# Second attention of a decoder layer: transposes of q, k and the attention weights go from TensorE to VectorE and ScalarE

## The chip, the cores and the metric

The kernel runs on one core of a Trainium2 chip. The metric is the time of one execution on the device, in microseconds. One of the executions is recorded by the hardware profiler; it gives the profile and the trace. The engines have short names: PE is TensorE's matmul, PEld its weight load, DVE is VectorE, ACT is ScalarE, POOL is GpSimd and SP issues most of the DMAs.

## The reference, cut to what matters

One hybrid decoder layer in float32, with 256 positions, a width of 2048 and 8 heads in each of two attentions. The change is in the second attention alone. Its block length equals the sequence length, so no other block is ever chosen, and what is left is causal attention with ALiBi:

```python
x = x + 0.5 * swiglu(rmsnorm(x, g_ffn1), w_ffn1_gu, w_ffn1_down)
h = rmsnorm(x, g_mix)
qa, ka, va, qb, kb, vb, gate_a, gate_b = split(h @ w_in)      # 3*1024, 3*1024, 2048, 2048 columns
o_a = diff_attention(qa, ka, va, lam, ...)                    # the first attention, 8 heads
# moba_attention, the second: per head of 128 columns, for this shape
s = q @ k.T * 128 ** -0.5                                     # 256 x 256
s = where(dist >= 0, s - slope * dist, -inf)
o_b = softmax(s) @ v
merged = sigmoid(gate_a) * (o_a @ p_a) + sigmoid(gate_b) * (o_b @ p_b)
x = x + merged @ w_o
x = x + 0.5 * swiglu(rmsnorm(x, g_ffn2), w_ffn2_gu, w_ffn2_down)
return rmsnorm(x, g_final)
```

## The kernel before, in words

The 256 positions lie in two tiles of 128 partitions. Each large product (`products`) streams its weight matrix from HBM in blocks of 512 columns. Every float32 weight tile `raw` is split into a high part `wh` (a copy by ScalarE, L103) and a low part `wl` (a difference by VectorE, L104), two row tiles of 128 at a time, and three matmuls per row tile and position tile add up in PSUM (L131 to L133). So one pair `wh`, `wl` feeds 12 matmuls. There are four `wh` buffers and three `wl` buffers, so ScalarE can run four pairs ahead of TensorE, and VectorE three. The text counts the work in these pairs.

The small work of the attentions is put between the matmuls of the large products. A queue `work` holds functions; `products` runs one of them after every fourth row tile (every two pairs), except at the start of a product. A product of 2048 rows has 8 pairs and three such steps. The framework's scheduler then orders each engine's instructions; an engine runs its list in order, and `wh` and `wl` are put forward by a priority.

In the steps around the change:
- While the q and k columns of the second attention are computed (`qkv`, four products for q and k), the eight heads of the first attention run in the steps. After each of these four products VectorE scales 512 columns into `qk`, and a piece of work is put at the head of the queue: `put_rows` transposes `qk` by eight TensorE transposes (`flipped`, L178) into PSUM tiles `tr`, and ScalarE copies them to their place (L214). The piece has 4 heads of q or k.
- Each head of the first attention (`diff_head`) takes four steps: scores and softmax; transpose of the weights `a`; the product with v, `o`, whose rows ScalarE scales to `on` (L343); and a transpose of `on`, which ScalarE and VectorE split into `oah` and `oal`. `tr` and `o` share two PSUM buffers: the transposes of `a` use the buffer that `oal` must have read.
- While the gate columns are computed, the eight heads of the second attention run (`moba_head`). In step i TensorE does the scores `sc` of head i, and two steps later the product `o` with v. In between VectorE adds ALiBi and takes the maxima (`s`, `top`, L304 to L308), ScalarE does the exponentials (L312), and VectorE takes `inv` and scales the weights to `a` (L359, L362). In the next step three TensorE transposes and one ScalarE copy (`flip_weights`, L178 and L319) make `aT`. After `o` ScalarE and VectorE split it into `obh` and `obl`. `sc` has one PSUM buffer, `aT` and `a` have two.

Elsewhere the kernel already transposes by VectorE: `turned` makes a full transpose of 128x512 from 16 transposes of 32x256, each from one group of 32 partitions to another (L193).

Of the kernel before, what the change touches and what calls it, by code (L numbers as in the profile page):

```python
# [24 lines left out]
F32 = mybir.dt.float32  # L25
F32R = mybir.dt.float32r
AF = mybir.ActivationFunctionType
# [3 lines left out]
P = 128  # L31
S = 256
T = S // P
# [4 lines left out]
Q = 32  # L38
# [9 lines left out]
def layer(ctx: ExitStack, tc: tile.TileContext, x_in, g_ffn1, w_gu1, w_down1, g_mix, w_in, lam_q1,  # L48
          lam_k1, lam_q2, lam_k2, g_subln, p_a, p_b, w_o, g_ffn2, w_gu2, w_down2, g_final, out):
    nc = tc.nc  # L50
    keep = ctx.enter_context(tc.tile_pool(name="keep", bufs=1))
    wp = ctx.enter_context(tc.tile_pool(name="wp", bufs=1))
    tp = ctx.enter_context(tc.tile_pool(name="tp", bufs=1))
# [46 lines left out]
    def split(hi, lo, src, scale=None):  # L100

        if scale is None:
            a = nc.scalar.activation(hi, src, AF.Copy)  # L103
            b = nc.vector.tensor_tensor(lo, src, hi.bitcast(F32), op=ALU.subtract)  # L104
        else:
            a = nc.scalar.activation(hi, src, AF.Copy, scale=scale)  # L106
            b = nc.vector.scalar_tensor_tensor(lo, src, scale, hi.bitcast(F32), op0=ALU.mult, op1=ALU.subtract)
        return a.ins, b.ins
# [61 lines left out]
    def product(lhs, w, n0, nk, apart=0):  # L170
        return products(lhs, w, [n0], nk, apart=apart)[0]

    def flipped(src):

        n = src.shape[-1] // P
        tr = psum.tile([P, n * P], F32, name="tr", tag="tr", bufs=2)
        for i in range(n):
            nc.tensor.transpose(tr[:, i * P:(i + 1) * P], src[:, i * P:(i + 1) * P], ident)  # L178
        return tr

    def both_tiles(name):

        return tp.tile([P, T, NB], F32, name=name, tag="h", bufs=1)
# [25 lines left out]
        i, k = divmod(k, size)  # L209
        return [part[:, k:k + n, t * P:(t + 1) * P] for part in lhs[i]]  # L210

    def put_rows(dst, both):
        for t in range(T):
            nc.scalar.activation(dst[:, :, t * P:(t + 1) * P],  # L214
                                 flipped(both[:, t]).rearrange("p (k q) -> p k q", k=4), AF.Copy)

    def put_turned_rows(dst, rows):
        for t in range(T):
# [75 lines left out]
    def weights(h, maps, qT, kT):  # L294

        n = len(maps)
        sc = psum.tile([P, n, NB], F32, name="sc", tag="sc", bufs=1)
        for m, rows in enumerate(maps):
            nc.tensor.matmul(sc[:, m, :P], qT[rows, h, :P], kT[rows, h, :P], start=True, stop=True)  # L299
        for m, rows in enumerate(maps):  # L300
            nc.tensor.matmul(sc[:, m, P:3 * P], qT[rows, h, P:], kT[rows, h, :], start=True, stop=True)  # L301
        s = tp.tile([P, n, 3 * P], F32, name="s", tag="s", bufs=2)
        slope = 2.0 ** (-8.0 * (h + 1) / HEADS)
        nc.vector.scalar_tensor_tensor(s, dist[:, None, :].to_broadcast([P, n, 3 * P]), slope, sc[:, :, :3 * P],  # L304
                                       op0=ALU.mult, op1=ALU.add)
        top = tp.tile([P, 2, n], F32, name="top", tag="top", bufs=2)
        nc.vector.tensor_reduce(top[:, 0, :], s[:, :, :P], axis=AX.X, op=ALU.max, negate=True)
        nc.vector.tensor_reduce(top[:, 1, :], s[:, :, P:], axis=AX.X, op=ALU.max, negate=True)  # L308
        total = tp.tile([P, 2, n], F32, name="total", tag="total", bufs=2)
        for m in range(n):  # L310
            for t, cols in enumerate((slice(0, P), slice(P, 3 * P))):
                nc.scalar.activation(s[:, m, cols], s[:, m, cols], AF.Exp, bias=top[:, t, m:m + 1],  # L312
                                     accum_out=total[:, t, m:m + 1])
        return s, total

    def flip_weights(a):

        aT = tp.tile([P, 3 * P], F32, name="aT", tag="aT", bufs=2)
        nc.scalar.activation(aT, flipped(a), AF.Copy)  # L319
        return aT  # L320

    def diff_head(h, qT, kT, v, lam, on, oT):
        p, total = weights(h, (slice(0, 64), slice(64, 128)), qT, kT)
        inv = tp.tile([P, T, 2], F32, name="inv", tag="inv", bufs=2)
        nc.vector.reciprocal(inv, total)

        c = tp.tile([P, T, 1], F32, name="c", tag="c", bufs=2)
        nc.vector.scalar_tensor_tensor(c, inv[:, :, 1:2], lam, total[:, :, 0:1], op0=ALU.mult, op1=ALU.mult)
        a = tp.tile([P, 3 * P], F32, name="a", tag="a", bufs=2)
        for t, cols in enumerate((slice(0, P), slice(P, 3 * P))):  # L330
            nc.vector.scalar_tensor_tensor(a[:, cols], p[:, 1, cols], c[:, t], p[:, 0, cols],
                                           op0=ALU.mult, op1=ALU.add)
        yield
        aT = flip_weights(a)
        yield
        o = psum.tile([P, T, P], F32, name="o", tag="tr", bufs=2)
        hc = slice(h * P, (h + 1) * P)
        nc.tensor.matmul(o[:, 0], aT[:, :P], v[:, 0, hc], start=True, stop=True)
        nc.tensor.matmul(o[:, 1], aT[:, P:2 * P], v[:, 0, hc], start=True, stop=False)
        nc.tensor.matmul(o[:, 1], aT[:, 2 * P:], v[:, 1, hc], start=False, stop=True)  # L340
        ss = tp.tile([P, T, 1], F32, name="oss", tag="oss", bufs=2)
        for t in range(T):
            nc.scalar.activation(on[:, t], o[:, t], AF.Copy, scale=inv[:, t, 0:1])  # L343
            sq = tp.tile([P, P], F32, name="osq", tag="osq", bufs=1)
            nc.vector.scalar_tensor_tensor(sq, on[:, t], 1.0, on[:, t], op0=ALU.mult, op1=ALU.mult,
                                           accum_out=ss[:, t])
        r = tp.tile([P, T, 1], F32, name="orms", tag="orms", bufs=2)
        nc.vector.tensor_scalar(ss, ss, 1.0 / P, EPS, op0=ALU.mult, op1=ALU.add)
        nc.gpsimd.tensor_tensor(r[:, :, 0], ss[:, :, 0], half.to_broadcast([P, T]), op=ALU.pow)
        for t in range(T):  # L350
            nc.vector.tensor_scalar(on[:, t], on[:, t], r[:, t], 1.0 - LAM_INIT, op0=ALU.mult, op1=ALU.mult)
        yield
        (hi, lo), = oT
        split(hi[:, h], lo[:, h], flipped(on.rearrange("p t d -> p (t d)")), scale=gsub)

    def moba_head(h, qT, kT, v, oT):
        p, total = weights(h, (slice(0, P),), qT, kT)
        inv = tp.tile([P, T, 1], F32, name="inv1", tag="inv", bufs=2)
        nc.vector.reciprocal(inv, total)  # L359
        a = tp.tile([P, 3 * P], F32, name="a1", tag="a", bufs=2)  # L360
        for t, cols in enumerate((slice(0, P), slice(P, 3 * P))):
            nc.vector.tensor_scalar(a[:, cols], p[:, 0, cols], inv[:, t], None, op0=ALU.mult)  # L362
        yield
        aT = flip_weights(a)
        yield
        o = psum.tile([P, S], F32, name="o1", tag="tr", bufs=2)
        hc = slice(h * P, (h + 1) * P)
        nc.tensor.matmul(o, v[:, 0, hc], aT[:, :S], start=True, stop=False)  # L368
        nc.tensor.matmul(o[:, P:], v[:, 1, hc], aT[:, S:], start=False, stop=True)  # L369
        (hi, lo), = oT  # L370
        split(hi[:, h], lo[:, h], o)

    def qkv(xT, rstd, n0, dim, tag):

        all_ = keep.tile([P, 3, HEADS * S], F32, name=f"qkv_{tag}", tag=tag)
        qT, kT = (all_[:, i].rearrange("p (h q) -> p h q", h=HEADS) for i in range(2))
        v = all_[:, 2].rearrange("p (t n) -> p t n", t=T)
        rq = []
        for t in range(T):
            rq.append(tp.tile([P, 1], F32, name="rq", tag="rq", bufs=2))  # L380
            nc.vector.tensor_scalar(rq[t], rstd[t], dim ** -0.5, None, op0=ALU.mult)
        for i, (dst, r) in enumerate(((qT, rq), (kT, rstd))):
            for b in range(W // NB):
                y = product(xT, w_in[0], n0 + i * W + b * NB, KD)
                hs = both_tiles("qk")
                for t in range(T):
                    nc.vector.tensor_scalar(hs[:, t], y[t], r[t], None, op0=ALU.mult)
                if work:
                    put_piece = partial(put_rows, dst[:, 4 * b:4 * b + 4], hs)
                else:  # L390
                    put_piece = partial(put_turned_rows, dst[:, 4 * b:4 * b + 4], turned(hs))
                work.appendleft(put_piece)
        for b in range(W // NB):
            y = product(xT, w_in[0], n0 + 2 * W + b * NB, KD)
            for t in range(T):
                nc.scalar.activation(v[:, t, b * NB:(b + 1) * NB], y[t], AF.Copy, scale=rstd[t])
        return qT, kT, v
# [155 lines left out]
```

## Time and profile before

| | us |
|---|---|
| median of three runs | 2110.7 (2110.1 to 2110.76) |
| profiled execution, its own time | 2111.54 |
| its span, first to last instruction | 2109.7 |
| PE busy in the span | 2091.8 (99%) |
| DVE busy | 1380.0 (65%) |
| ACT busy | 983.5 (47%) |

The three runs agree within 0.03%. The profiled execution is 0.84 us above the median, and its own time is 1.84 us more than its span. Matmuls are pipelined, so two that follow each other overlap in the record; the distance of their starts is what one costs the engine. Busy shares are averages over stages with different limits.

### The profile page before, as it was taken

The page shows a single profiled execution, that of the slowest core. Times are in us where ns is not written, and L with a number is a line of the kernel's source. Part 1 is how long each engine was busy: PE and PEld are TensorE (multiplying, and loading weights), DVE is VectorE, ACT ScalarE, POOL GpSimd, SP SyncE. Part 2 cuts the span into 40 slices and gives each one's busy share as a digit, 9 for nine tenths or more (in the row PEclk, how much of TensorE's full clock was granted, in tenths as well). Part 3 has the DMA queues.
Part 4 walks back from the last instruction along what each step waited for, and adds up shares of the span by engine and source line. Part 5 has one row for each costly group of instructions (what it writes and reads, how often), then busy time and mean ns, then how long its engine had stood idle before and what let it go on. Part 6 is the DMA issues. An engine that isn't in the chain of part 4 may idle for free.

```text
span 2109.7 us, 24363 instructions
## 1 busy us (share of the span) xinstructions
PE 2091.8 (99%) x9330; PEld 1729.4 (82%) x9330; DVE 1380.0 (65%) x1846; ACT 983.5 (47%) x1224; POOL 13.6 (1%) x26
## 2 busy tenths in 40 slices
PE   8999999999999999999999999999999999999998
PEld 7888888888888888778888888888888888888886
DVE  5676664466678887675554489977766644666754
ACT  6544443344445544555564534554444433444443
POOL 0000000000000000000000000000000000000000
PEclk9999999999999999999999999999999999999999
DMA  7556655565555556545545555565565556556563
GB/s 244 198 181 200 198 194 188 196 199 187 193 199 190 191 192 201 166 153 167 180 160 193 187 197 194 187 219 194 185 199 200 184 195 199 191 189 199 180 200 138
DMA packets 201799, 401.25 MB, mean 190 GB/s; under 512 B 6945, under 2 KB 6994, under 8 KB 201554
## 3 DMA queue, kind: packets, MB, share of 16 engines
q1 hardware_dynamic: 201584, 399.66, 57.3%
q8 instruction: 73, 1.20, 0.2%
q14 instruction: 44, 0.36, 0.0%
q10 hardware_dynamic: 98, 0.03, 0.0%
HBM read 397.57 MB, written 2.10 MB: 189 GB/s over the span
## 4 chain that ended last, share of the span: by engine, by line
PE 98%; ACT 1%; DVE 0%; DMA 0%; issue 0%; ACTq 0%; SPq 0%; POOLq 0%; POOL 0%; DVEq 0%
PE acc L131 32%; PE acc L133 32%; PE acc L132 32%; PE tr L178 1%; ACT wh L103 0%; DMA raw<-in_w_ffn_gu_dram 0%; PE sc L301 0%; PE o L368 0%; DVE wl L104 0%; PE sc L299 0%; ACT on L343 0%; ACT oah L106 0%; PE o L369 0%; ACT sq L243 0%; DVE rows L193 0%
## 5 line engine op out<-in xcount | busy, mean ns | idle before, releaser
L104 DVE TENSOR_TENSOR wl<-raw,wh 128x1024 fp32r<-128x1024 f32 x752 | 918.1, 1224 | 619.7 <-PE acc L132 558.2
L103 ACT ACTIVATE wh<-raw 128x1024 fp32r<-128x1024 f32 x752 | 796.6, 1060 | 914.7 <-PE acc L133 889.2
L131 PE MATMUL acc<-wh,xTh 128*128 128x512 f32 x1472 | 577.5, 393 | 2.2 <-ACT xTh L106 2.2
L133 PE MATMUL acc<-wh,xTl 128*128 128x512 f32 x1472 | 574.4, 390 | 0.2 <-DVE xTl L104 0.2
L132 PE MATMUL acc<-wl,xTh 128*128 128x512 f32 x1472 | 573.8, 390 | 0.0
L131 PEld LDWEIGHTS acc<-wh,xTh 128*128 128x128 f32 x1472 | 277.4, 188 | 60.4 <-ACT xTh L106 2.6
L133 PEld LDWEIGHTS acc<-wh,xTl 128*128 128x128 f32 x1472 | 276.9, 188 | 58.5 <-DVE xTl L104 0.6
L132 PEld LDWEIGHTS acc<-wl,xTh 128*128 128x128 f32 x1472 | 277.0, 188 | 57.0
L132 PE MATMUL acc<-wl,bigh 128*128 128x512 f32 x704 | 274.0, 389 | 0.0
L131 PE MATMUL acc<-wh,bigh 128*128 128x512 f32 x704 | 273.7, 389 | 0.0
L133 PE MATMUL acc<-wh,bigl 128*128 128x512 f32 x704 | 273.7, 389 | 0.0
L131 PE MATMUL acc<-wh,oah 128*128 128x512 f32 x416 | 161.8, 389 | 0.0
L132 PE MATMUL acc<-wl,oah 128*128 128x512 f32 x416 | 161.8, 389 | 0.0
L133 PE MATMUL acc<-wh,oal 128*128 128x512 f32 x416 | 161.8, 389 | 0.0
L131 PE MATMUL acc<-wh,obh 128*128 128x512 f32 x416 | 161.8, 389 | 0.0
L132 PE MATMUL acc<-wl,obh 128*128 128x512 f32 x416 | 161.8, 389 | 0.0
L133 PE MATMUL acc<-wh,obl 128*128 128x512 f32 x416 | 161.8, 389 | 0.0
L193 DVE STREAM_TRANSPOSE rows<-h 32x256 f32<-32x256 f32 x352 | 153.5, 436 | 6.4
L132 PEld LDWEIGHTS acc<-wl,bigh 128*128 128x128 f32 x704 | 132.2, 188 | 27.7 <-DVE wl L104 0.4
L133 PEld LDWEIGHTS acc<-wh,bigl 128*128 128x128 f32 x704 | 132.2, 188 | 27.5
L131 PEld LDWEIGHTS acc<-wh,bigh 128*128 128x128 f32 x704 | 132.2, 188 | 27.4
L133 PEld LDWEIGHTS acc<-wh,obl 128*128 128x128 f32 x416 | 78.1, 188 | 16.2
(116 smaller groups left out, 1056.5 us busy)
## 6 DMA issues: line engine op xcount, KB each, us to landing
raw<-in_w_ffn_gu_dram SPq DMA_DIRECT2D x174, 1024.0 KB, 5.1
raw<-in_w_ffn_down_dram SPq DMA_DIRECT2D x88, 1024.0 KB, 5.0
raw<-in_w_in_dram SPq DMA_DIRECT2D x80, 1024.0 KB, 5.1
raw<-in_w_o_dram SPq DMA_DIRECT2D x16, 1024.0 KB, 5.1
raw<-in_p_a_dram SPq DMA_DIRECT2D x8, 1024.0 KB, 5.2
raw<-in_p_b_dram SPq DMA_DIRECT2D x8, 1024.0 KB, 5.1
x<-in_x_dram SPq DMA_DIRECT2D x8, 256.0 KB, 5.9
raw<-in_w_ffn_gu_dram SPq DMA_DIRECT2D x4, 512.0 KB, 6.5
```

The source lines that it names most:

```text
L103: a = nc.scalar.activation(hi, src, AF.Copy)
L104: b = nc.vector.tensor_tensor(lo, src, hi.bitcast(F32), op=ALU.subtract)
L131: nc.tensor.matmul(acc[t], hi, wh, start=(k == 0), stop=False)
L132: nc.tensor.matmul(acc[t], hi, wl, start=False, stop=False)
L133: return nc.tensor.matmul(acc[t], lo, wh, start=False, stop=(k == nk - 1)).ins
L178: nc.tensor.transpose(tr[:, i * P:(i + 1) * P], src[:, i * P:(i + 1) * P], ident)
L193: nc.vector.transpose(rows[c * Q:(c + 1) * Q, a], both[a * Q:(a + 1) * Q, c])
```

## The change

For q and k of the second attention, `squares_of` replaces the eight TensorE transposes of a piece by two VectorE instructions over all 128 partitions, each of which transposes every 32x32 square in place of its group of partitions (128x512 elements, L218 after). `put_squares` then moves the squares to their partitions by 16 ScalarE copies of 32 partitions x 256 elements (L226), where there were two of 128x512 from PSUM. `squares` takes the one buffer `rows` that `turned` uses.

For the weights of the second attention, `turn_weights` makes `aT` with 16 VectorE transposes of 32 partitions x 96 elements (three squares each, L339), each from one group of partitions of `a` to another of `aT`. The three TensorE transposes and the ScalarE copy of a head are gone. The first attention keeps them.

```diff
-    def put_rows(dst, both):
-        for t in range(T):
-            nc.scalar.activation(dst[:, :, t * P:(t + 1) * P],
-                                 flipped(both[:, t]).rearrange("p (k q) -> p k q", k=4), AF.Copy)
+    def squares_of(both):
+        squares = tp.tile([P, 4, T, 4, Q], F32, name="squares", tag="rows", bufs=1)
+        for t in range(T):
+            nc.vector.transpose(squares[:, :, t], both[:, t].rearrange("p (k c j) -> p c k j", c=4, j=Q))
+        return squares
+
+    def put_squares(dst, squares):
+        for a in range(4):
+            for c in range(4):
+                part = dst[c * Q:(c + 1) * Q].rearrange("p k (t a i) -> p t k a i", t=T, i=Q)[:, :, :, a]
+                nc.scalar.activation(part, squares[a * Q:(a + 1) * Q, c], AF.Copy)
...
+    def turn_weights(a):
+        aT = tp.tile([P, 3, 4, Q], F32, name="aT", tag="aT", bufs=2)
+        a = a.rearrange("p (b c j) -> p c b j", c=4, j=Q)
+        for q in range(4):
+            for c in range(4):
+                nc.vector.transpose(aT[c * Q:(c + 1) * Q, :, q], a[q * Q:(q + 1) * Q, c])
+        return aT.rearrange("p b q i -> p (b q i)")
...
-        aT = flip_weights(a)
+        aT = turn_weights(a)
...
-                    put_piece = partial(put_rows, dst[:, 4 * b:4 * b + 4], hs)
+                    put_piece = partial(put_squares, dst[:, 4 * b:4 * b + 4], squares_of(hs))
```

Line numbers after the change are higher by 11 to 20 from `squares_of` on: L304 becomes L315, L359 becomes L379, and so on.

The first place is ScalarE at the first q piece, while heads of the first attention run. Before:

```order
L103 ACTIVATE wh<-raw 128x1024 x3
L214 ACTIVATE qkv_bigl<-tr 128x4x128 x2
L103 ACTIVATE wh<-raw 128x1024 x2
L106 ACTIVATE oah<-tr,gains 128x256
L343 ACTIVATE on<-o,inv 128x128 x2
```

Now:

```order
L103 ACTIVATE wh<-raw 128x1024 x2
L226 ACTIVATE qkv_bigl<-squares 32x2x4x32 x2
L103 ACTIVATE wh<-raw 128x1024
L226 ACTIVATE qkv_bigl<-squares 32x2x4x32 x6
L103 ACTIVATE wh<-raw 128x1024
L226 ACTIVATE qkv_bigl<-squares 32x2x4x32 x5
L103 ACTIVATE wh<-raw 128x1024
L226 ACTIVATE qkv_bigl<-squares 32x2x4x32 x3
L106 ACTIVATE oah<-tr,gains 128x256
L363 ACTIVATE on<-o,inv 128x128 x2
```

The 16 copies stand between the last `wh` before `oah`, in the second and third piece as 4, 6, 5 and 1.

The second place is VectorE at the fourth head of the second attention, from its maxima to the next head. Before:

```order
L307 TENSOR_REDUCE top<-s 128x1
L308 TENSOR_REDUCE top<-s 128x1
L104 TENSOR_TENSOR wl<-raw,wh 128x1024
L359 RECIPROCAL inv_7777<-total 128x2
L362 TENSOR_SCALAR a_7779<-s,inv_7777 128x128
L362 TENSOR_SCALAR a_7779<-s,inv_7777 128x256
L104 TENSOR_TENSOR wl<-raw,wh 128x1024
L104 TENSOR_TENSOR obl<-o_7816,obh 128x256
```

Now:

```order
L318 TENSOR_REDUCE top<-s 128x1
L319 TENSOR_REDUCE top<-s 128x1
L104 TENSOR_TENSOR wl<-raw,wh 128x1024
L379 RECIPROCAL inv_7838<-total 128x2
L382 TENSOR_SCALAR a_7840<-s,inv_7838 128x128
L382 TENSOR_SCALAR a_7840<-s,inv_7838 128x256
L104 TENSOR_TENSOR wl<-raw,wh 128x1024
L339 STREAM_TRANSPOSE aT<-a_7840 32x3x32 x3
L104 TENSOR_TENSOR obl<-o_7877,obh 128x256
L339 STREAM_TRANSPOSE aT<-a_7840 32x3x32 x13
L104 TENSOR_TENSOR wl<-raw,wh 128x1024
```

The 16 transposes stand in VectorE's list between the same `wl` as before, ahead of the next head.

The third place is TensorE at the step in which the product `o` of the third head stands. Before:

```order
L133 MATMUL acc_7720<-wh,xTl 128x512
L368 MATMUL o_7816<-aT,qkv_bigl 128x256
L369 MATMUL o_7816<-aT,qkv_bigl 128x128
L178 MATMUL tr<-ident,a_7779 128x128 x3
L299 MATMUL sc<-qkv_bigl 128x128
L301 MATMUL sc<-qkv_bigl 128x256
```

Now:

```order
L133 MATMUL acc_7770<-wh,xTl 128x512
L388 MATMUL o_7877<-aT,qkv_bigl 128x256
L389 MATMUL o_7877<-aT,qkv_bigl 128x128
L310 MATMUL sc<-qkv_bigl 128x128
L312 MATMUL sc<-qkv_bigl 128x256
```

The three transposes are gone, and each `o` stands behind as many matmuls of the large product as before.

## Rows read from the trace of the kernel before

**Rows 1.** The page, part 1: busy us, share of the span, instructions.

```profile
PE 2091.8 (99%) x9330; PEld 1729.4 (82%) x9330; DVE 1380.0 (65%) x1846; ACT 983.5 (47%) x1224; POOL 13.6 (1%) x26
```

**Rows 2.** Window: length; PE, PEld, DVE, ACT, POOL busy (instructions); clock; DMA.

```profile
900.00:920.00 20.00, 19.38 (x104) 15.64 (x103) 15.90 (x37) 12.38 (x30) 1.39 (x2) 1.00 0.39 121
```

**Rows 3.** Timeline of PE at the first q piece: start, duration.

```profile
896.39 0.40 PE L133 MATMUL acc<-wh,xTl 128*128 128x512 f32 x1
896.62 1.04 PE L178 MATMUL tr<-ident,qk 128*128 128x128 f32 x8
...
897.73 0.39 PE L132 MATMUL acc<-wl,xTh 128*128 128x512 f32 x1
```

**Rows 4.** Timeline of PE, heads of the second attention.

```profile
1025.02 0.38 PE L299 MATMUL sc<-qkv_bigl 128*128 128x128 f32 x2
...
1031.15 0.49 PE L178 MATMUL tr<-ident,a 128*128 128x128 f32 x3
...
1031.47 0.39 PE L299 MATMUL sc<-qkv_bigl 128*128 128x128 f32 x2
...
1091.22 0.59 PE L368 MATMUL o<-aT,qkv_bigl 128*128 128x256 f32 x2
...
1103.13 0.59 PE L368 MATMUL o<-aT,qkv_bigl 128*128 128x256 f32 x2
```

**Rows 5.** Groups of DVE by form: count, busy, mean ns, idle before.

```profile
L104 DVE TENSOR_TENSOR wl<-raw,wh 128x1024 fp32r<-128x1024 f32 x752 | 918.1, 1224 | 619.7 <-PE acc L132 558.2 <-issue 39.8 <-ACT wh L103 10.8
...
L104 DVE TENSOR_TENSOR bigl<-rows,bigh 128x512 fp32r<-128x512 f32 x44 | 30.2, 688 | 6.5 <-ACT bigh L103 6.5
L193 DVE STREAM_TRANSPOSE rows<-qk 32x256 f32<-32x256 f32 x64 | 27.9, 436 | 1.1
```

**Rows 6.** Timeline of DVE, at transposes and at a head's start.

```profile
454.31 2.23 DVE L193 STREAM_TRANSPOSE rows<-h 32x256 f32<-32x256 f32 x5
...
1025.05 1.23 DVE L104 TENSOR_TENSOR wl<-raw,wh 128x1024 fp32r<-128x1024 f32 x1 [1.50 <-PE acc L132]
1026.19 0.55 DVE L304 SCALAR_TENSOR_TENSOR s<-dist,sc 128x384 f32<-128x384 f32 x1
```

**Rows 7.** Window of seven heads of the second attention, columns as in rows 2.

```profile
1026.20:1086.00 59.80, 59.80 (x290) 50.39 (x289) 36.70 (x67) 40.11 (x72) 0.00 (x0) 1.00 0.51 164
```

**Rows 8.** Waits in 1020 to 1110 us: total, times, longest.

```profile
DVE inv L359 <- ACT s L312: 5.7, 8, 0.8
```

**Rows 9.** Groups of ACT by form, columns as in rows 5.

```profile
L103 ACT ACTIVATE wh<-raw 128x1024 fp32r<-128x1024 f32 x752 | 796.6, 1060 | 914.7 <-PE acc L133 889.2 <-DMA raw<-in_w_ffn_gu_dram 5.3 <-issue 5.1
...
L219 ACT ACTIVATE qkv_bigh<-rows 128x512 f32<-128x512 f32 x8 | 5.0, 625 | 14.9 <-DVE rows L193 14.9
L343 ACT ACTIVATE on<-o,inv 128x128 f32<-128x128 f32 x16 | 4.9, 361 | 0.0
```

**Rows 10.** Timeline at the step behind the first q piece.

```profile
902.97 0.38 PE L178 MATMUL tr<-ident,on 128*128 128x128 f32 x2
...
903.17 1.06 ACT L103 ACTIVATE wh<-raw 128x1024 fp32r<-128x1024 f32 x1 [1.61 <-PE acc L133]
...
904.13 0.46 ACT L106 ACTIVATE oah<-tr,gains 128x256 fp32r<-128x256 f32 x1
...
904.49 0.61 ACT L343 ACTIVATE on<-o,inv 128x128 f32<-128x128 f32 x2
904.62 0.48 DVE L107 SCALAR_TENSOR_TENSOR oal<-tr,gains,oah 128x256 fp32r<-128x256 f32 x1 [0.40 <-ACT oah L106]
...
905.15 0.55 PE L178 MATMUL tr<-ident,a 128*128 128x128 f32 x3 [0.28 <-ACT on L343]
```

**Rows 11.** Timeline of PE at the start of the kernel.

```profile
9.71 0.63 PE L133 MATMUL acc<-wh,xTl 128*128 128x512 f32 x1
10.14 0.63 PE L131 MATMUL acc<-wh,xTh 128*128 128x512 f32 x1
...
13.55 0.63 PE L133 MATMUL acc<-wh,xTl 128*128 128x512 f32 x1
```

## The prediction

> **What bounds the kernel now.** First the busy times: PE is busy for 99% of the span [rows 1], so what it no longer does is time won, and every wait put on it is time lost. Then the two stages of the change, by windows. While q and k of the second attention are computed, PE has small gaps and VectorE is the next busiest, at 15.9 of 20 us in the fullest window [rows 2]. While the heads of the second attention run, PE has no gap, and VectorE is busy for 36.7 of 59.8 us [rows 7]. Last the timelines, for what one step costs on the engine that bounds, and for how close the others are behind it.
>
> **What PE saves.** A matmul of the large products starts 0.23 us after the one before. Around the eight transposes of a piece, the step from the transposes to the second matmul behind them is 897.73 - 896.62 = 1.11 us where 0.23 would stand [rows 3]: 0.88 for eight, 3.5 us for four pieces. The three transposes of a head push the scores from 1031.15 to 1031.47 [rows 4]: 0.32, 2.6 us for eight heads. Together 6.1 us. The records show 0.33 us and more for one transpose, but they overlap, so the starts count.
>
> **The squares on VectorE.** Eight instructions of 128x512. By the rate of the rows, 1224 - 688 = 536 ns for 512 elements [rows 5], one is 436 + 256 x 1.047 = 0.70 us; two per piece, 5.6 us in all. They stand between the scaling of `qk` and the next `wl` but one, in a stage where VectorE has 4 of 20 us free [rows 2] and runs three pairs ahead. I cost them at nothing; without that cover they cost 5.6.
>
> **The copies on ScalarE.** A copy of 128x1024 takes 1060 ns and one of 128x512 625 [rows 9], so 256 columns take 0.41 us. Two `on` of 0.361 take 0.61 together [rows 10]: the second starts 0.11 before the first ends. No row has copies that change partitions; the bounds are a start every 0.30 us (they overlap like `on`) and every 0.41 (they don't). I take 0.30, for the rows of the same engine show the overlap. A piece then takes 4.8 us where about 1.06 stood. ScalarE waits 1.6 us ahead of a `wh` [rows 10], so groups of 5 and 6 copies fill these gaps, and `oah` behind them is late. Whoever waits: `oal`, then the buffer `tr`, then the transposes of `a` on PE, which already wait there from about 904.70 to 905.15 [rows 10]. By adding up ScalarE's list of the first piece from 0.65 us after the end of pair 322 (896.62), when the squares are ready (2 copies, `wh`, 6, `wh`, 5, `wh`, 3), `oah` starts at 8.4 us, `oal` ends at 9.35, and PE, which now has four matmuls ahead of the transposes, is there at 8.2. That is a wait of 1.2 where 0.45 stood. In the second and third piece one copy stands behind the last `wh`, and I get 0.1 more each; behind the fourth piece no transposes of `a` follow. Sum 1.0; since each lateness also moves `on` and the exponentials, I take 1.5. With a start every 0.41 the same addition gives 2.4 + 1.9 + 1.9 = 6.2.
>
> **The weights on VectorE: the term that decides.** 128 transposes of 32x96. A transpose of 32x256 takes 436 ns [rows 5], and five start 2.23 / 5 = 0.446 apart [rows 6]: they don't overlap, unlike the `s` that starts 0.09 before its `wl` ends [rows 6]. At the measured rate, 160 elements less are 0.168 less: 0.268, one start every 0.28 us. Bounds: proportional to the elements, 0.164 (0.174 apart), and no shorter than 32x256, 0.446 apart. I take 0.28, since `wl` and its half show a fixed part (1224 is less than twice 688). That is 4.5 us per head on an engine that has to give 1.2 us per pair besides.
>
> [...]
>
> PE needs `aT` of head 7 at its product `o`. Scores of head 1 start at 1025.02, that `o` at 1091.22 [rows 4]; without seven groups of transposes it would be due 66.2 - 2.2 = 64.0 us after them. VectorE's list up to the last transpose of head 7: `s` of head 1 starts 1.2 us in [rows 4, 6]; seven heads with 18 `wl` and six `obl` are the window's 36.7 [rows 7]; one more `wl` 1.2; 112 transposes x 0.28 = 31.4; the overlap that an instruction loses beside transposes, 0.09 at two places a head, 1.3; and waits for exponentials. Those were 5.7 over eight heads [rows 8], 5.0 for seven. Now a `wl` stands in the gap in most heads, but on ScalarE a `wh` stands between the two exponentials in several; I take half, 2.5 (bounds 0 and 5). Sum 74.3: `o` of head 7 waits until VectorE is 10.3 us behind. On the way `o` of heads 4 and 6 take part of that as waits of their own, and `sc` waits where `s` of the head before is late. Behind it PE has 11.9 - 0.3 = 11.6 us to the last `o` [rows 4] and VectorE one head with three `wl`, 2.2 + 4.5 + 3.7 + 0.5 = 10.9: no more is added.
>
> **Sum.** -6.1 + 1.5 + 10.3 = +5.7 us. The profiled execution is 2111.54 by its own time on a span of 2109.7, so its like would be 2117.2 on 2115.4. The median of the runs is 0.84 lower: 2110.7 + 5.7 = 2116.4.
>
> **Rivals.**
> - **The transposes are short and VectorE keeps up.** Nothing is late where a start comes every 0.19 us (0.28 - 10.3 / 112). At the lower bound the sum is -6.1 + 1.5 = -4.6: 2106.1. For it: nothing here is as short. Against it: the fixed part. [...]
> - **The copies don't overlap on ScalarE.** Instead of 1.5 the pieces cost 6.2: 2121.1. For it: transposes between groups of partitions don't overlap on VectorE [rows 6]. Against it: that is another engine.
> - **The transposes are long.** At 0.446 apart, 112 x 0.166 = 18.6 more: 2135.0; at 0.31, 3.4 more: 2119.8. Against it: the measured rate.
> [...]
>
> **How the numbers follow.** Chances: forecast 0.60, its own range 2113 to 2120 (waits for exponentials 0 to 5 us, transposes 15 ns either way); short transposes 0.12; copies without overlap 0.14; long transposes 0.07; the clock 0.05; 0.02 for less than I see. I count 0.2%, 4.2 us, as the least that a measurement of this kernel can tell from no change: 2106.5 to 2114.9. About a quarter of the forecast (0.16), half of the short transposes (0.06) and 0.03 of the rest fall within; 0.07 fall below it; 0.68 above. The range 2108 to 2123 leaves out 0.08 below and some 0.10 above.
>
> **What the profile after would show.** PE: no L178 for `qk`, 24 fewer for `a`; about 10 us of idle time between 1040 and 1100, before `o` of heads 4, 6 and 7, put down to transposes on VectorE (L339), whose mean is 0.27. VectorE nearly full from head 1 to 8, its total 128 x 0.27 + 5.6 = 40 us higher. ScalarE: 64 copies of 0.4. The waits of `tr<-a` behind the pieces about 1 us longer. If L339 is below 0.19, or if PE does not wait at `o`, the forecast is wrong; if `tr` waits over 2 us behind each piece, the second rival holds.

## The result, and the profile after

The changed kernel takes 2129.95 us (median of 4 runs, 2128.85 to 2131.78), the kernel before 2110.62 beside it on the same chip: 1.0091 times as long, 95% interval 1.0079 to 1.0103, 19.3 us more. The predicted direction was right; the time lies 7 us above the range.

The first part of the page of after, in the columns of [rows 1], on a span of 2128.3 us:

```profile
PE 2094.9 (98%) x9274; PEld 1728.4 (81%) x9274; DVE 1417.4 (67%) x1982; ACT 1002.2 (47%) x1272; POOL 13.6 (1%) x26
```

PE has 56 instructions less and its busy time is 3.1 us longer. Its mean granted clock over the run, by the view of the cores, is 0.995, where before had 0.999:

```profile
core 0: 2128.3 us, clock 0.995
```

Where the time went is told by windows of the two stages; columns as in [rows 2]. Before:

```profile
885.00:1010.00 125.00, 123.43 (x613) 101.11 (x613) 81.17 (x152) 66.54 (x126) 5.54 (x8) 1.00 0.49 158
1010.00:1130.00 120.00, 120.00 (x559) 100.36 (x559) 65.00 (x95) 71.41 (x110) 0.00 (x0) 1.00 0.52 172
```

After:

```profile
885.00:1010.00 125.00, 115.00 (x536) 92.53 (x536) 80.13 (x154) 85.06 (x177) 5.53 (x8) 0.96 0.43 143
1010.00:1130.00 120.00, 113.12 (x498) 92.99 (x497) 94.61 (x220) 61.37 (x95) 0.00 (x0) 0.97 0.48 158
...
900.00:920.00 20.00, 16.41 (x83) 12.73 (x83) 11.34 (x30) 14.48 (x36) 1.39 (x2) 0.91 0.32 107
```

The first stretch holds q and k of the second attention beside the heads of the first, the second the heads of the second. PE is idle for 10 and for 6.9 us in them (before 1.6 and 0), and beside that the granted clock is 0.96 and 0.97. The last row is the stretch of [rows 2], where the clock was 1.00.

The waits of PE in the first stage and (below the dots) in the second, from the view of waits of after (total us, times, longest):

```profile
PE tr L178 <- ACT on L363: 9.5, 5, 3.2
PE tr L178 <- DVE on L371: 0.5, 1, 0.5
...
PE o L388 <- DVE aT L339: 5.8, 2, 2.9
PE sc L310 <- DVE s L315: 1.1, 2, 0.9
```

In before the first of these lines was

```profile
PE tr L178 <- ACT on L343: 1.5, 5, 0.3
```

(the 0.28 of [rows 10] is one of its five), and the other three had nothing. In after three of the five are long, one behind each of the first three pieces (3.25, 2.77 and 2.77 us by the timeline). The 0.5 us of the second line is a wait of the transposes of `on` behind the fourth piece. The timeline of PE at the first, after:

```profile
908.16 0.61 PE L178 MATMUL tr<-ident,a 128*128 128x128 f32 x3 [3.25 <-ACT on L363]
908.47 0.74 PE L132 MATMUL acc<-wl,xTh 128*128 128x512 f32 x1
909.00 0.63 PE L133 MATMUL acc<-wh,xTl 128*128 128x512 f32 x1
909.43 0.63 PE L131 MATMUL acc<-wh,xTh 128*128 128x512 f32 x1
...
911.56 0.57 PE L133 MATMUL acc<-wh,xTl 128*128 128x512 f32 x1
911.97 0.39 PE L131 MATMUL acc<-wh,xTh 128*128 128x512 f32 x1
912.20 0.39 PE L132 MATMUL acc<-wl,xTh 128*128 128x512 f32 x1
```

Behind the wait the matmuls start 0.43 us apart, as at the start of the kernel [rows 11], and go back to 0.23 at 911.97. The granted clock of 900 to 920 is 0.91: the wait is paid twice.

What the wait is for stands in ScalarE's timeline of after, to be read beside [rows 10]:

```profile
902.62 2.12 ACT L226 ACTIVATE qkv_bigl<-squares 32x256 f32<-32x256 f32 x5
904.76 1.06 ACT L103 ACTIVATE wh<-raw 128x1024 fp32r<-128x1024 f32 x1
905.84 1.26 ACT L226 ACTIVATE qkv_bigl<-squares 32x256 f32<-32x256 f32 x3
907.12 0.47 ACT L106 ACTIVATE oah<-tr,gains 128x256 fp32r<-128x256 f32 x1
907.49 0.62 ACT L363 ACTIVATE on<-o,inv 128x128 f32<-128x128 f32 x2
```

Five copies take 2.12 us, three 1.26: a start every 0.43, and even the `wh` starts 0.02 after the last copy has ended. `oah` starts at 907.12 and the transposes of `a` end their wait 1.04 later.

The heads of the second attention, to be read beside [rows 4], in PE's timeline of after: the scores of head 1, the `o` of head 7 and that of head 8.

```profile
1035.14 0.38 PE L310 MATMUL sc<-qkv_bigl 128*128 128x128 f32 x2
...
1108.44 0.70 PE L388 MATMUL o<-aT,qkv_bigl 128*128 128x256 f32 x2 [2.88 <-DVE aT L339]
...
1121.74 0.59 PE L388 MATMUL o<-aT,qkv_bigl 128*128 128x256 f32 x2
```

The `o` of head 7 waits for VectorE's transposes, which last as long as reckoned, by the view of L339 in after (in ns the least, the median and the most):

```profile
L339 DVE STREAM_TRANSPOSE aT<-a x128: 255/270/276, 1040.2 to 1119.4; 32x96 f32<-32x96 f32 x128
```

The scores of head 1 now start 10.1 us later; from there to the last `o` it is 86.6 us, 8.5 more. Together that is the 18.6 us by which the spans of the two profiled executions differ (2128.3 and 2109.7), so the rest of the kernel takes as long as before. Each part comes out of three numbers, to within 0.6 us. First stage: 3.5 saved, 8.5 more waiting (9.5 and 0.5, against 1.5), and 125 x 0.04 = 5.0 of clock: +10.0. Second: 2.6 saved, 6.9 waiting, 120 x 0.03 = 3.6 of clock: +7.9.

### The profile page after: what moved, and what is told of

Read it like the earlier page. It is cut to its first block, busy times and chain, and to the rows that moved or that the text cites. A ratio compares the mean times of both kernels' runs of the same rounds, so it can differ in the third digit from the quotient of the medians.

```text
span 2128.3 us, 24423 instructions
## 1 busy us (share of the span) xinstructions
PE 2094.9 (98%) x9274; PEld 1728.4 (81%) x9274; DVE 1417.4 (67%) x1982; ACT 1002.2 (47%) x1272; POOL 13.6 (1%) x26
## 4 chain that ended last, share of the span: by engine, by line
PE 94%; ACT 2%; DVE 2%; issue 0%; DMA 0%; ACTq 0%; POOL 0%; SPq 0%; POOLq 0%; DVEq 0%
PE acc L131 31%; PE acc L132 31%; PE acc L133 31%; ACT qkv_bigl L226 1%; DVE aT L339 1%; ACT wh L103 1%; DVE wl L104 1%; PE tr L178 0%; DMA raw<-in_w_ffn_gu_dram 0%; PE sc L312 0%; ACT on L363 0%; ACT oah L106 0%; PE sc L310 0%; DVE s L315 0%; PE o L388 0%
## 5 line engine op out<-in xcount | busy, mean ns | idle before, releaser
L132 PEld LDWEIGHTS acc<-wl,obh 128*128 128x128 f32 x416 | 78.1, 188 | 16.2
```

The costliest lines, as they stand in the source:

```text
L132: nc.tensor.matmul(acc[t], hi, wl, start=False, stop=False)
```

## The experiments

**The two halves.** E1 keeps the change for q and k and gives the weights back to TensorE; E2 is the reverse, with `put_rows` as it was before.

```diff
-        aT = turn_weights(a)
+        aT = flip_weights(a)
```

> The squares and copies of q and k alone; the weights stay on TensorE. [...] Rival B (the low clock comes from both halves of the change together, and the waits alone act here): three waits of 2.8 us less 3.5 saved, 2115.5 with a full clock.

Measured: 2121.47, ratio 1.0050 (1.0033 to 1.0067).

```diff
-                    put_piece = partial(put_squares, dst[:, 4 * b:4 * b + 4], squares_of(hs))
+                    put_piece = partial(put_rows, dst[:, 4 * b:4 * b + 4], hs)
```

> The weights by VectorE alone; q and k stay on TensorE. Theory A (VectorE's list from head 1 to head 7 is about 10 us too long, and waits of some 3 us at o of heads 4 and 7 lower the clock a little): the heads' stage loses 8.5 us as in the changed kernel, 2119.1. Rival B (without the first half there is no low clock, and part of the loss goes): 2116 to 2117.

Measured: 2119.07, ratio 1.0039 (1.0024 to 1.0054). The two add up: 10.6 and 8.2 us over before make 18.8, against 19.3. PE's waits are those of after to within 0.1 us, 9.5 and 0.5 in E1 and 5.7 and 1.1 in E2. So no sign is left that the halves feed each other, and each can be studied alone. The windows of E1, then of E2:

```profile
885.00:1010.00 125.00, 114.99 (x536) 92.71 (x535) 80.01 (x154) 84.93 (x177) 5.54 (x8) 0.96 0.43 143
1010.00:1130.00 120.00, 120.00 (x559) 100.36 (x558) 64.97 (x95) 69.52 (x107) 0.00 (x0) 1.00 0.51 169
```

```profile
885.00:1010.00 125.00, 123.42 (x615) 101.36 (x614) 80.61 (x148) 66.05 (x124) 5.55 (x8) 1.00 0.48 158
1010.00:1130.00 120.00, 113.22 (x498) 93.08 (x497) 94.59 (x220) 62.88 (x98) 0.00 (x0) 0.97 0.47 158
```

Both times rival B fails: the clock falls in the stage whose half is in, to 0.96 in E1 and 0.97 in E2, and is 1.00 in the other.

**Fewer copies on ScalarE.** E3 is E1 with four of a piece's 16 copies on GpSimd, E4 with all 16.

```diff
-                nc.scalar.activation(part, squares[a * Q:(a + 1) * Q, c], AF.Copy)
+                if a < 3:
+                    nc.scalar.activation(part, squares[a * Q:(a + 1) * Q, c], AF.Copy)
+                else:
+                    nc.gpsimd.tensor_copy(part, squares[a * Q:(a + 1) * Q, c])
```

> As e1, but four of the 16 copies of a piece are done by GpSimd. Theory A: ScalarE is through 1.7 us earlier, the waits of a's transposes shrink to 1 to 1.5 us, too short for the clock to fall: 5.1 us from the waits and about 5 us from the clock, 2110 to 2111, with a granted clock of 0.999. Rival B (the clock does not fall because of the waits, but for lower activity in the stage): only the 5.1 us, 2115.6, and the granted clock of the stage stays near 0.93.

Measured: 2112.09, ratio 1.0007 (0.9998 to 1.0016). The first long wait is 2.54 us, and the matmuls behind it start 0.43 apart for a while (theory A had no wait so long, and the time is 1.1 us above its range); another is 1.28, and behind that one they go on at 0.23. PE's timeline of E3 at the two:

```profile
905.74 0.55 PE L178 MATMUL tr<-ident,a 128*128 128x128 f32 x3 [2.54 <-ACT on L366]
...
935.42 0.55 PE L178 MATMUL tr<-ident,a 128*128 128x128 f32 x3 [1.28 <-ACT on L366]
935.73 0.48 PE L131 MATMUL acc<-wh,xTh 128*128 128x512 f32 x1
936.04 0.40 PE L132 MATMUL acc<-wl,xTh 128*128 128x512 f32 x1
936.27 0.39 PE L133 MATMUL acc<-wh,xTl 128*128 128x512 f32 x1
```

Four copies off ScalarE, some 1.7 us a piece, give back 9 us of the 10.6.

```diff
-                nc.scalar.activation(part, squares[a * Q:(a + 1) * Q, c], AF.Copy)
+                nc.gpsimd.tensor_copy(part, squares[a * Q:(a + 1) * Q, c])
```

> As e1, but all 16 copies of a piece are done by GpSimd. Theory A: ScalarE has less to do than before, the waits are what they were before the change, and TensorE keeps the 3.5 us: 2107.1. Rival B (the squares on VectorE are late, whoever copies): over 2113. Rival C (GpSimd's copies are long and hold up its small power instruction for the norm of the first attention): a wait for on instead, 2115 or more.

Measured: 2107.60, ratio 0.9984 (0.9975 to 0.9994): less than the kernel before. All ten runs (2107.06 to 2108.24) lie below all nineteen of before beside them (2110.18 to 2111.88), though the 3.4 us by the ratio are less than the 4.2 that the prediction counted as tellable from no change. GpSimd needs longer for the copies than ScalarE, 9.77 us for the 16 of the first piece against 6.8 in after, but close behind them stands only one short instruction (`orms`). Its timeline in E4:

```profile
896.03 9.77 POOL L226 COPY qkv_bigl<-squares 32x256 f32<-32x256 f32 x16 [10.81 <-DVE squares L218]
```

PE waits 2.1 us in the stage, as in before 1.5: 3.5 saved and 0.6 lost make 2.9; the ratio gives 3.4. So the prediction's price of the transposes of q and k stands, and so does that of the squares, which cost nothing.

**Is it the wait that the clock falls for?** E5 is E1 with 24 matmuls more where TensorE waits, behind the `o` of heads 2, 4 and 6 of the first attention; nothing reads their product.

```diff
-        o = psum.tile([P, T, P], F32, name="o", tag="tr", bufs=2)
+        o = psum.tile([P, T + 1, P], F32, name="o", tag="tr", bufs=2)
...
+        if h in (1, 3, 5):
+            for _ in range(24):
+                nc.tensor.matmul(o[:, 2], ident, ident, start=True, stop=True)
```

> E1 again, with 24 matmuls of 128x128 (about 0.22 us each, 5.3 us) added after the o of the heads that run beside each of the first three pieces; their product is never read. They stand where TensorE waits for ScalarE's copies, and the scores and four matmuls that stood there (1.6 us) come behind them. Theory A, the clock falls because TensorE stands still for some 3 us: no wait over 1 us is left, the granted clock of 885 to 1010 us goes from 0.96 back to 0.99 or 1.00, and the 15.9 us of added work cost next to nothing: 2121 us (E1 2121.5, plus 3 x 1.6, less the 5 us of the clock). Theory B, the clock falls for another reason (ScalarE's and VectorE's copies, whatever TensorE does): 0.96 as in E1, and about 2126 us.

Measured: 2123.72, ratio 1.0061 (1.0046 to 1.0076). The windows of E5:

```profile
885.00:1010.00 125.00, 123.79 (x670) 103.63 (x671) 79.42 (x153) 83.02 (x175) 5.53 (x8) 1.00 0.41 137
```

ScalarE and VectorE do what they did in E1, TensorE has no wait over 1 us, and the clock is back at 1.00. On the clock theory A holds. The time does not tell by itself: it lies 2.7 us above A's and 2.3 below B's. By their starts the added matmuls take 5.4 us a piece, 16.1 in all. The waits in the stage fall by 8.8 us (from 9.5 and 0.5 in E1 to 0.7 and 0.5), so 7.3 us of the work lie outside the waits, where A had reckoned with 4.8. Less the 5.0 that the clock gave back, that makes 2.3, and the span is 2.3 us longer than E1's (2121.9 against 2119.6).

**Why the copies do not overlap.** Four variants of E1's loop, in which only the partitions (sets of 32) that a copy reads and writes differ.

```diff
-                part = dst[c * Q:(c + 1) * Q].rearrange("p k (t a i) -> p t k a i", t=T, i=Q)[:, :, :, a]
+                part = dst[a * Q:(a + 1) * Q].rearrange("p k (t a i) -> p t k a i", t=T, i=Q)[:, :, :, c]
```

> E1 again, but each of the 16 copies of a piece writes the partitions that it reads, in the order of before; q and k stand in wrong places, so only the time is read. Neither input nor output changes its partitions from a copy to the next three. Theory A, ScalarE's copies of 32x256 do not overlap because each goes to other partitions than the last: they now start about 0.30 us apart like the 128x128 copies of rows 9 and 10, 16 take 4.8 us instead of 6.8, the waits for them fall from 3.3 to about 1.3 us, the clock stays, and the time is 2110 to 2112 us. Theory B, a copy of this size and stride takes 0.43 us whatever partitions it goes to: 2121 to 2122 us, waits of 3.3 us.

Measured: 2111.63, ratio 1.0003 (0.9994 to 1.0012). ScalarE's timeline of E6, with two starts taken apart:

```profile
898.20 2.06 ACT L226 ACTIVATE qkv_bigl<-squares 32x256 f32<-32x256 f32 x6
...
898.50 0.40 ACT L226 ACTIVATE qkv_bigl<-squares 32x256 f32<-32x256 f32 x1
...
898.91 0.42 ACT L226 ACTIVATE qkv_bigl<-squares 32x256 f32<-32x256 f32 x1
```

The six are copies 3 to 8. Copy 4 starts 0.30 after copy 3, on the same partitions; copy 5 goes to the next 32 and starts 0.41 after copy 4.

```diff
-        for a in range(4):
-            for c in range(4):
+        for c in range(4):
+            for a in range(4):
```

> E1 again, with the loops over the copies exchanged: four copies in a row write the same 32 partitions and read another 32 each time (E1: the output's change each time, the input's every fourth). If the change of the output's partitions hinders the overlap: starts 0.30 us apart within four, 0.33 on the mean, waits near 1.7 us, 2111 to 2114 us. If the change of the input's, or neither: 0.43 apart, 2121 to 2122 us.

Measured: 2121.81, ratio 1.0051 (1.0036 to 1.0066); the output stays, the input changes. In E1 it is the other way round, so a change of either is enough. In ScalarE's timeline of E7 the same six:

```profile
899.32 2.55 ACT L226 ACTIVATE qkv_bigl<-squares 32x256 f32<-32x256 f32 x6
```

E6 and E7 leave open whether the change from copy to copy hinders, or the move to other partitions within a copy. E9 moves every copy by one set and keeps both for four; E10 moves none and changes both each time.

```diff
-                part = dst[c * Q:(c + 1) * Q].rearrange("p k (t a i) -> p t k a i", t=T, i=Q)[:, :, :, a]
+                part = dst[(a + 1) % 4 * Q:((a + 1) % 4 + 1) * Q].rearrange("p k (t a i) -> p t k a i", t=T, i=Q)[:, :, :, c]
```

> E1 again, but each of the 16 copies of a piece reads one set of 32 partitions and writes the next one (0 to 1, 1 to 2, 2 to 3, 3 to 0), four in a row alike; q and k stand in wrong places, so only the time is read. E6 had neither a change from copy to copy nor a move within a copy. Theory A, what hinders the overlap is that input or output changes its partitions from one copy to the next: as in E6, starts 0.33 us apart on the mean, waits under 1.8 us, 2111 to 2112 us. Theory B, what hinders it is that a copy writes other partitions than it reads: all 16 move, 0.43 apart, waits of 3.3 us, clock 0.96, 2121 to 2122 us.

Measured: 2114.16, ratio 1.0014 (1.0004 to 1.0023).

```diff
-                nc.scalar.activation(part, squares[a * Q:(a + 1) * Q, c], AF.Copy)
+                nc.scalar.activation(part, squares[c * Q:(c + 1) * Q, a], AF.Copy)
```

> E1 again, but each copy writes the partitions that it reads, and the next copy goes to the next 32; q and k stand in wrong places, so only the time is read. Theory A (the change from copy to copy hinders the overlap): 0.43 apart, 2121 to 2122 us. Theory B (the move within a copy hinders it): 0.30 to 0.33 apart, 2110.5 to 2112 us.

Measured: 2120.70, ratio 1.0045 (1.0030 to 1.0060). The six in ScalarE's timelines, E9 and then E10:

```profile
897.88 2.08 ACT L226 ACTIVATE qkv_bigl<-squares 32x256 f32<-32x256 f32 x6
```

```profile
898.21 2.56 ACT L226 ACTIVATE qkv_bigl<-squares 32x256 f32<-32x256 f32 x6
```

It is the change: 0.43 apart in E1, E7 and E10, 0.33 on the mean in E6 and E9, with the move or without. E9's time was 2 us above what theory A expected. In E6 a `wh` (128 partitions, from the first on) and a copy of the first 32 still overlap, by ScalarE's timeline by 0.09 us:

```profile
896.61 0.73 ACT L226 ACTIVATE qkv_bigl<-squares 32x256 f32<-32x256 f32 x2 [1.99 <-DVE squares L218]
897.25 1.04 ACT L103 ACTIVATE wh<-raw 128x1024 fp32r<-128x1024 f32 x1
```

E9's copies, which read and write different sets, overlap with no `wh`, and its waits are a little longer. The first, in PE's timelines of E6 and then E9:

```profile
906.31 0.55 PE L178 MATMUL tr<-ident,a 128*128 128x128 f32 x3 [1.80 <-ACT on L363]
```

```profile
906.02 0.55 PE L178 MATMUL tr<-ident,a 128*128 128x128 f32 x3 [2.07 <-ACT on L363]
...
964.01 0.55 PE L178 MATMUL tr<-ident,a 128*128 128x128 f32 x3 [1.55 <-ACT on L363]
```

The clock of the stretch 900 to 920 falls to 0.91 in E9, which it does not in E6. It falls again at 960 to 980, behind a wait of 1.55 us (the last line above), though E6 kept its clock behind 1.80. So the length of a wait alone does not decide whether the clock falls; what else does is not settled here. The windows of the two stretches, E6 and then E9:

```profile
900.00:920.00 20.00, 17.86 (x97) 14.12 (x96) 14.31 (x37) 15.13 (x39) 1.39 (x2) 1.00 0.34 111
960.00:980.00 20.00, 18.52 (x90) 14.72 (x89) 14.46 (x32) 11.55 (x24) 1.38 (x2) 1.00 0.40 135
```

```profile
900.00:920.00 20.00, 17.59 (x89) 13.71 (x88) 13.00 (x33) 14.15 (x37) 1.38 (x2) 0.91 0.32 106
960.00:980.00 20.00, 18.40 (x88) 14.48 (x87) 13.00 (x30) 11.83 (x27) 1.38 (x2) 0.91 0.41 134
```

**The weights by one transpose.** E8 is E4 and the second attention's weights off TensorE in another way.

```diff
+        squares = tp.tile([P, 4, 3, Q], F32, name="wsq", tag="wsq", bufs=1)
+        nc.vector.transpose(squares, a.rearrange("p (b c j) -> p c b j", c=4, j=Q))
         aT = tp.tile([P, 3, 4, Q], F32, name="aT", tag="aT", bufs=2)
-        a = a.rearrange("p (b c j) -> p c b j", c=4, j=Q)
         for q in range(4):
             for c in range(4):
-                nc.vector.transpose(aT[c * Q:(c + 1) * Q, :, q], a[q * Q:(q + 1) * Q, c])
+                src, out = squares[q * Q:(q + 1) * Q, c], aT[c * Q:(c + 1) * Q, :, q]
+                if c % 2:
+                    nc.scalar.activation(out, src, AF.Copy)
+                else:
+                    nc.gpsimd.tensor_copy(out, src)
```

> E4 (q and k with all copies on GpSimd, weights on TensorE) and the second attention's weights off TensorE too, by one VectorE transpose of 128x384 (about 0.57 us) and 16 copies of 32x96, eight on GpSimd and eight on ScalarE, which are 8 x 0.3 to 0.4 us in two lists side by side. Theory A, the heads' stage was late in the change because VectorE was full (18.3 to 18.9 of 20 us): VectorE's list is 3.9 us per head shorter, no wait for the weights over 1 us, the clock 1.00, and the 2.6 us of TensorE's transposes are gained: 2105 to 2106 us. Theory B, it was the time from a to the turned weights: the copies take 2.4 to 4 us behind the transpose, about the 4.5 us of the change, and the stage stays some 8 us late: 2113 to 2116 us.

Measured: 2108.53, ratio 0.9988 (0.9979 to 0.9998), between the two theories. What they ask shows in the windows of the heads' stage, after and then E8:

```profile
1060.00:1080.00 20.00, 16.00 (x73) 12.92 (x73) 18.86 (x49) 12.19 (x22) 0.00 (x0) 0.98 0.42 137
```

```profile
1060.00:1080.00 20.00, 19.94 (x94) 16.80 (x95) 12.11 (x21) 17.34 (x37) 6.69 (x17) 1.00 0.47 157
```

VectorE goes from 18.9 to 12.1 of 20 us, and the clock stays. The way of one head's weights is shorter by less. For head 8 the transpose starts at 1087.98 and the last of GpSimd's eight copies ends 4.8 us later, by the timeline of E8:

```profile
1087.98 0.58 DVE L336 STREAM_TRANSPOSE wsq<-a 128x384 f32<-128x384 f32 x1
...
1088.72 4.11 POOL L344 COPY aT<-wsq 32x96 f32<-32x96 f32 x8 [1.42 <-DVE wsq L336]
```

That is more than the 4.5 us that 16 transposes take by themselves, and less than the 5.8 of head 7 in the change, where a `wl` stands among them (1102.61 to 1108.39). So it was above all VectorE's full list that made the heads' stage late. Of the 2.6 us that TensorE saves, though, 2.1 go into new waits for GpSimd at two `o`, by the waits of E8:

```profile
PE o L393 <- POOL aT L344: 2.1, 2, 1.2
```

E8 and E4 can't be told apart by time (2108.53 and 2107.60, each within 1 us or so). E4 is the simpler of the two that beat the kernel before.

## Why the prediction was wrong

- **What PE saves, 6.1 us:** 3.5 for q and k stands by E4. The 2.6 of the weights was measured only within sums (E2, E8), which agree with it.
- **The squares at nothing:** right; 0.70 us each, as reckoned, and no wait of PE is put down to them.
- **The copies, +1.5: the step that failed.** I took a start every 0.30 us, from the two `on` of [rows 10], which run on the same 128 partitions. The copies change partitions each time and start every 0.43, above even the upper bound of 0.41, since they do not start before the last has ended. The second rival had this, with 6.2 us and a chance of 0.14. The sign that it named came true, waits over 2 us behind each of the first three pieces. But the measured waits grew by 8.5, not 6.2. The first piece's list, from its first copy to `oah`, took 10.1 us (897.0 to 907.12) where 16 x 0.41 and three `wh` of 1.06 make 9.7: every instruction there starts 0.01 to 0.02 after the last has ended, the `wh` too. Three times 0.4 is half of the 2.3 that the rival lacked; 0.5 more is the wait of `on` behind the fourth piece, where the prediction had none, and the last 0.6 are not taken apart.
- **The clock: a chance of 0.05, and nothing in the sum.** In after its fall came behind waits of 2.8 to 3.3 us, at all three pieces and at two `o` in the heads' stage: 5.0 and 3.6 us by the windows. In E9 it came behind 2.07 and 1.55 too. E5 shows that in the first stage it is the waits that it falls for; in the heads' stage that is argued from the same pattern, and from E8, where the longest wait is 1.21 us and the clock stays at 1.00. Even with the copies at the second rival's price, 4.7 more, the sum would have made 2121.1, not 2129.95.
- **The weights, +10.3:** 0.268 us each was predicted, and the transposes' median is 0.270. E2 gives 8.2 us for this half, the prediction's 10.3 - 2.6 = 7.7. The mechanism held: from the scores of head 1 to `o` of head 7, which waits for VectorE, the prediction's list makes 74.3 us, and 73.3 were measured. The rest is in part luck. Behind that `o` nothing was to be added to 11.6 us, and it took 13.3 to the last `o`, with matmuls 0.43 us apart from 1110.31 to 1112.87 and a clock of 0.91 in 1100 to 1120: 1.0 less and 1.7 more nearly cancel. PE's waits stand at `o` of heads 4 and 7, not 4, 6 and 7, and at two of the scores, and sum to 6.9, not 10.3.
- **The sum:** 5.7, plus 7.0 of waits and 5.0 of clock in the first stage, plus 0.5 in the second, is 18.2. Measured were 19.3 between the medians, of which 0.7 is not in the spans of the two profiled executions (18.6), from which the waits and the clock were read; the 0.4 left is not settled.

## What to carry to other kernels

A piece of work given to another engine is priced by its place in that engine's list: with q and k's copies on ScalarE, ahead of a step that TensorE waits for, the kernel lost 10.6 us, and with the same copies on GpSimd, which takes longer for them but is otherwise idle, it won 3.4. An overlap read off one pair of instructions holds for pairs of that kind; check whether the partitions stay the same (0.30 us apart in E6, 0.43 in E1). And a wait of two or three microseconds put on a busy TensorE is priced with the slower matmuls that may follow it (0.43 us apart for 0.23 in after; the clock fell behind 1.55 us too, and not behind every wait of that size): 8.5 us of added waits came to 13.5.

## What the runs showed of the hardware

- On ScalarE, 32-partition copies start 0.30 to 0.33 us apart while input and output stay on the same partitions (E6, E9), and only when the last has ended once either changes (0.43 apart and 0.415 long in E1, E7 and E10, 0.41 apart in E6). VectorE's transposes of 32x96 in after, whose output changes its partitions each time, start 0.28 apart and are 0.270 long.
- Inside a busy stage the granted clock of a stretch of 20 us fell to 0.91 behind waits of TensorE of 1.55 and 2.07 (E9), 2.54 (E3) and 3.25 us (after). Behind the last three the matmuls of 512 columns started 0.43 us apart for a while. Behind waits of 1.28 (E3), 1.58 (E9) and 1.80 (E6) it stayed at 1.00, and they went on 0.23 apart. The ranges overlap, so the length alone does not decide.
- On GpSimd a copy of 32x256 has a median of 0.396 us and a longest of 1.431, and 16 of them take 9.77 (E4), where 16 medians would make 6.3. For 32x96 (E8) the median is 0.260, the longest 1.312, and eight take 4.11 where eight medians would make 2.1. Why is not settled.
